# A long convolution by tables in rounded parts, its halves of the frequencies stepped one behind the other

## The chip, the cores and the metric

The kernel runs on one core of one Trainium2 chip. What counts is the device time of one execution in microseconds (us), taken as the median of several runs. Beside the runs one execution is recorded by the hardware profiler; all rows below come from it. The engines: TensorE (PE; PEld is its loading of weights), VectorE (DVE), ScalarE (ACT), GpSimd (POOL), SyncE (SP); the DMA queues that an engine feeds bear its name.

## The reference

Two layers of a backbone with a width of 1024. 512 latent tokens and 128 context tokens (640 columns in all) go through each: a gated feed-forward part, a mixer, and a second feed-forward part. The mixer splits its input between pooling, windowed attention, and an order-2 Hyena of 256 channels, whose long convolution is what the change concerns:

```python
def fft_conv(z, k):
    """z (B, L, C), k (2L, C): bidirectional convolution over the whole sequence via zero padding to 2L."""
    L = z.shape[1]
    zf = jnp.fft.rfft(z, n=2 * L, axis=1)
    kf = jnp.fft.rfft(k, n=2 * L, axis=0)
    return jnp.fft.irfft(zf * kf[None], n=2 * L, axis=1)[:, :L]

def hyena_mixer(u, sw, sb, filt, bias_d):
    uc = short_conv(u, sw, sb).astype(F32)
    v, x1, x2 = jnp.split(uc, 3, axis=-1)
    bd = bias_d.astype(F32)
    z = v
    for o, gate in enumerate((x1, x2)):
        z = gate * (fft_conv(z, filt[:, o]) + bd[o] * z)
    return z.astype(u.dtype)
```

So each layer has two long convolutions, the second on the gated result of the first.

## The kernel before

The tokens lie along the free dimension. Every large product is made in two halves of 320 columns, and as three products of rounded parts: an operand is split into a rounded `hi` (ScalarE, L294) and the rest `lo` (VectorE, L295), both of type float32r, and TensorE adds `hi*hi`, `lo*hi` and `hi*lo`. Weights come by DMA from SyncE as `raw`, are split into `whi` and `wlo`, and meet the activations `hhi`/`hlo` (or `ahi`, `phi`, ...).

In the mixer, several tasks share TensorE. Each is a generator, and a string `MIXP` (L32, walked at L1552) names the one whose next step is issued. `F` is the stream of the large products with `win` and `wout`; `A`, `X`, `Q`, `K`, `V` and `N` are attention, `P` pooling, and `C` is `hyena()`. TensorE keeps exactly the order in which its products are issued (L195 to L207); the other engines get theirs from the same program, and each engine works through its list in order. `F` asks for `C` itself once it needs its result (`phi` and `hhl`).

`C` has five steps for each of its two convolutions (`conv_step_old`, L1065), and an eleventh that splits the result into `yhi` and `ylo`:

1. The tables of the forward transform are requested (`load_full`, L256, by SyncE), the five tiles `kf` of the filter's transform are fetched, and the input is transposed on TensorE (`ztp`) and copied to `zt`.
2. The first half of the frequencies (`fi = 0`): 8 products `zf` with `zt`; ScalarE copies the odd part to `zod` (L1096), VectorE makes sum and difference `zp`, `zm`, multiplies each with the filter (`cmul`, tiles `cw` and `cy`, L966 to L971), and adds and subtracts into `pp` and `pmn` (L1104, L1105).
3. The same for `fi = 1`, then the request of the four back tables, and the context part (`zfc`, `zcs`).
4. 16 products `yt` of the back transform and the small `ytc`, scaled into `yv` by ScalarE.
5. The gate: `yu`, `yw` on VectorE.

The products of the convolution take f32 operands as they are: one instruction is one product, and the profile shows two records for it.

All these tiles, the tables among them, come from one pool of `SLOTS = 45` equal slots (`slot()`, `slot3()`), handed out in turn: whoever takes a slot waits until the last reader of its previous tile is done. The products of the convolution go to a pool of four PSUM banks (`mix`).

The program also has a second version of the step, `conv_step` (L974), which is chosen by `CONV3` (L1485) and which the kernel before does not use. It takes its tables by `load_tables` (L264); `triple` (L273) issues the three products. The program prints these functions:

Of the kernel before, what the change touches and what calls it, by code (L numbers as in the profile page):

```python
# [11 lines left out]
F32 = mybir.dt.float32  # L12
# [16 lines left out]
RCP = 300  # L29
RCP2 = 0  # L30
ORDER = "v0 v1 k q0 q1 q2 q3 xa xb v p0 p1 xc xd".split()
MIXP = "FCFFCFFFFFFCFNFCFKFFFFCQQFCQFFQFCPFFCPCFFAVAXAFAAFFCAPFXFAAPFAFFFAFFAAAFAAFFAAFAAAAXFAXFXAFFFFAFABFFBAABBFABAAFAAFFFFFFFF"  # L32
PROT = 8
AG0 = (1, 0, 2)
MIXT = 70
# [12 lines left out]
PVSKEW = 1  # L48
AHD = 2
PROP = "TGTTTTGGTGSGGGGTGTSTGTGTGSTGTGGSXTSGTSQGQDTGTQGGTTDDSTGTTQGSQGTDDTDTQQSGQQGQQDDQQDDDGTRQGSSDTSGDGGNDQNQSTTTGDGQDTSGQTDTGSGDDQGQDGTQSTQGDNGD"  # L50
CONV3 = 0
SQN = 3
TABX = 1
ADAW = (1.0, 1.25, 2.0, 0.75)
# [128 lines left out]
def hybrid_kernel(ctx: ExitStack, tc: tile.TileContext, a, depth=2, fc=22):  # L183
    nc = tc.nc
    V, S, G, DMA = nc.vector, nc.scalar, nc.gpsimd, nc.sync
# [78 lines left out]
    def load_tables(name, h, n, new=slot):  # L264

        ts = []
        for q in range(n):
            t = new(512, F32R, name="tab")
            DMA.dma_start(out=t.bitcast(F32), in_=a[name][h, q])
            ts.append(t.rearrange("p (h c f) -> p h c f", h=2, c=2))  # L270
        return ts

# [701 lines left out]
    def conv_step(l, o, z, gate, out):  # L974
        rl, rlc = filt[l]
        tf = [load_tables("fwd", 0, 4)]
        kf = filter_tiles(l, o)
        hb = PR(l, "hb")
# [15 lines left out]
        for fi in range(2):  # L994
            eo = []
            for pa in range(2):
                ps = mix(512, "zf")
                for c in range(2):
                    for i in range(2):
                        triple(ps[:, c * 256:(c + 1) * 256], [tf[fi][pa * 2 + i][:, h, c] for h in range(2)],  # L1000
                               [t[:, i, :] for t in zt[pa]], i == 0, i == 1)
                eo.append(ps)
            od = slot(512, name="zod")
            S.copy(out=od, in_=eo[1])
            zp, zm = slot(512, name="zp"), slot(512, name="zm")
            V.tensor_tensor(out=zp, in0=od, in1=eo[0], op=ALU.add)
            V.scalar_tensor_tensor(out=zm, in0=od, scalar=-1.0, in1=eo[0], op0=ALU.mult, op1=ALU.add)
            y = cmul(zp, kf[fi], o, 0)
            yp = cmul(zm, kf[2 + fi], o, 1)
            pp, pm_ = slot3(2, 256, name="pp"), slot3(2, 256, name="pmn")  # L1010
            for q in range(2):
                V.tensor_tensor(out=pp[:, q], in0=y[:, q], in1=yp[:, 1 - q], op=ALU.add)
                V.tensor_tensor(out=pm_[:, q], in0=y[:, q], in1=yp[:, 1 - q], op=ALU.subtract)
            hl = []
            for p_ in (pp, pm_):
                hl.append((slot3(2, 256, F32R, "ph"), slot3(2, 256, F32R, "pl")))
                split(p_, *hl[-1])
            pq.append(hl)
            if fi == 0:
                tf.append(load_tables("fwd", 1, 4))  # L1020
            if fi == 0:
                yield
        ti, vs = [load_tables("back", 0, 4)], []
        psc = mix(512, "zfc")
        for c in range(2):
# [119 lines left out]
    def short_conv(l, ci, u):  # L1145
        sw, sb = PR(l, "sw"), PR(l, "sb")
        t = slot(T, name="sc")
        S.activation(out=t, in_=u, func=AF.Identity, bias=sb[:, ci:ci + 1], scale=sw[:, 6 + ci:7 + ci])
        for c0, c1 in SEG:
            V.scalar_tensor_tensor(out=t[:, c0 + 1:c1], in0=u[:, c0:c1 - 1], scalar=sw[:, ci:ci + 1],  # L1150
                                   in1=t[:, c0 + 1:c1], op0=ALU.mult, op1=ALU.add)
            V.scalar_tensor_tensor(out=t[:, c0:c1 - 1], in0=u[:, c0 + 1:c1], scalar=sw[:, 12 + ci:13 + ci],
                                   in1=t[:, c0:c1 - 1], op0=ALU.mult, op1=ALU.add)
        return t
# [3 lines left out]
    def mixer(l, cur, nxt):  # L1158
# [90 lines left out]
        def need(name):  # L1249
            while name not in made:  # L1250
                next(stream)
            return made[name]
# [227 lines left out]
        def hyena():  # L1480
            zs = [short_conv(l, i, need(f"v{i}")) for i in range(2)]
            for o, (ci, ns) in enumerate(((2, ("xa", "xb")), (4, ("xc", "xd")))):
                out = []
                gate = lambda: [short_conv(l, ci + i, need(n)) for i, n in enumerate(ns)]
                yield from (conv_step if CONV3 else conv_step_old)(l, o, zs, gate, out)  # L1485
                zs = out
# [62 lines left out]
        def step(t):  # L1549
            next(tasks[t], None)  # L1550

        for t in MIXP.replace(" ", ""):  # L1552
            step(t)
# [253 lines left out]
```

## Time and profile before

| | |
|---|---|
| median of 3 runs | 2418.3 us |
| lowest and highest run | 2416.39 and 2420.72 us |
| the profiled execution, its own time | 2417.21 us |
| its span in the profile | 2415.4 us |
| TensorE busy | 2369.8 us, 98% |
| VectorE busy | 1920.3 us, 80% |
| ScalarE busy | 1094.6 us, 45% |
| GpSimd busy | 17.8 us, 1% |
| DMA, mean over the span | 112 GB/s |

The own time of the profiled execution includes what lies around its span, 1.8 us. Busy time is a sum over a stage with several limits; which engine sets the end of a stage is read from the waits and from the chain of work that ended last. Layer 0 has its mixer at about 560 to 860 us, layer 1 at about 1720 to 2020 us.

### The profile page before, as it was taken

The numbers are of one execution on the slowest core, as the hardware profiler recorded it, in microseconds if no ns is written. First come the engines' busy times: TensorE is split into PE (matmuls) and PEld (weight loads), VectorE is DVE, ScalarE is ACT, GpSimd is POOL, SyncE is SP. The second block draws the span as 40 slices with busy tenths as digits, with TensorE's granted clock in tenths as the row PEclk, the third lists the DMA queues.
The fourth block names the chain that finished last, engine by engine and source line by source line (L and its number), as shares of the span: only waits on it lengthen the run. The fifth ranks groups of instructions, "written<-read, shape, count | busy, mean of one in ns | idle before, by whom it ended". The sixth has DMA issues, their size and how long they took to land.

```text
span 2415.4 us, 41068 instructions
## 1 busy us (share of the span) xinstructions
PE 2369.8 (98%) x15576; PEld 2246.0 (93%) x15576; DVE 1920.3 (80%) x3885; ACT 1094.6 (45%) x2228; POOL 17.8 (1%) x46
## 2 busy tenths in 40 slices
PE   8999999999989999999999999999998999999999
PEld 3799999999877999999999999999987789999999
DVE  7887888986786798888889889898678678567583
ACT  4653352534345653443535435253434555335251
POOL 0000000000000000000000000000000000000000
PEclk9999999999989999999999999999998999999999
DMA  9434434353210235434343443534231022222222
GB/s 323 168 105 132 134 115 154 101 170 114 102 45 15 78 106 161 127 121 144 117 131 106 124 130 116 164 113 154 89 105 61 18 71 79 79 84 78 85 68 90
DMA packets 132646, 270.37 MB, mean 112 GB/s; under 512 B 15002, under 2 KB 24924, under 8 KB 132320
## 3 DMA queue, kind: packets, MB, share of 16 engines
q1 hardware_dynamic: 132448, 267.75, 34.5%
q8 instruction: 122, 2.00, 0.3%
q14 instruction: 76, 0.62, 0.1%
HBM read 259.56 MB, written 8.13 MB: 111 GB/s over the span
## 4 chain that ended last, share of the span: by engine, by line
PE 93%; DVE 4%; issue 1%; ACT 1%; DMA 1%; SPq 0%; POOL 0%; POOLq 0%; DVEq 0%; ACTq 0%
PE mm L204 79%; PE Z L204 5%; PE yt L204 1%; PE o L204 1%; PE pt L208 1%; PE fk L204 1%; PE mx L204 1%; PE ada L204 1%; PE zf L204 1%; PE rsb L204 0%; PE qbc L204 0%; DMA ar<-in_ada 0%; PE tot L204 0%; DMA par<-in_par 0%; PE nps L204 0%
## 5 line engine op out<-in xcount | busy, mean ns | idle before, releaser
L204 PE MATMUL mm<-hhi,whi 128*128 128x320 f32 x1440 | 448.2, 311 | 1.1 <-ACT u L1220 1.1
L204 PE MATMUL mm<-hlo,whi 128*128 128x320 f32 x1440 | 445.7, 309 | 0.0
L294 ACT CAST whi<-raw 128x512 fp32r<-128x512 f32 (+1 forms) x394 | 238.8, 607 | 456.2 <-PE mm L204 425.9
L204 PE MATMUL mm<-hhi,wlo 128*128 128x320 f32 x1440 | 445.4, 309 | 0.0
L204 PE MATMUL mm<-ahi,whi 128*128 128x320 f32 x1198 | 370.2, 309 | 0.0
L204 PE MATMUL mm<-alo,whi 128*128 128x320 f32 x1198 | 370.2, 309 | 0.0
L204 PE MATMUL mm<-ahi,wlo 128*128 128x320 f32 x1198 | 370.2, 309 | 0.0
L295 DVE TENSOR_TENSOR wlo<-raw,whi 128x512 fp32r<-128x512 f32 (+1 forms) x394 | 262.9, 670 | 77.4 <-ACT whi L294 75.2
L409 DVE CUSTOM_DVE_ANT_0 junk<-araw,condb,par 128x1024 bf16<-128x1024 f32 x240 | 307.1, 1280 | 2.2 <-DMA araw<-in_adat 0.7
L204 PEld LDWEIGHTS mm<-hhi,whi 128*128 128x128 f32 x1440 | 270.3, 188 | 6.0 <-ACT u L1220 2.8
L204 PEld LDWEIGHTS mm<-hlo,whi 128*128 128x128 f32 x1440 | 270.6, 188 | 2.0 <-issue 1.8
L204 PEld LDWEIGHTS mm<-hhi,wlo 128*128 128x128 f32 x1440 | 270.3, 188 | 1.4 <-issue 1.4
L204 PE MATMUL mm<-thi,whi 128*128 128x320 f32 x864 | 267.0, 309 | 0.0
L204 PE MATMUL mm<-tlo,whi 128*128 128x320 f32 x864 | 267.0, 309 | 0.0
L204 PE MATMUL mm<-thi,wlo 128*128 128x320 f32 x864 | 267.0, 309 | 0.0
L204 PEld LDWEIGHTS mm<-ahi,whi 128*128 128x128 f32 x1198 | 224.9, 188 | 0.0
L204 PEld LDWEIGHTS mm<-ahi,wlo 128*128 128x128 f32 x1198 | 224.9, 188 | 0.0
L204 PEld LDWEIGHTS mm<-alo,whi 128*128 128x128 f32 x1198 | 224.9, 188 | 0.0
L294 ACT CAST whi<-ex 128x512 fp32r<-128x512 f32 x216 | 134.2, 621 | 186.9 <-PE mm L204 173.3
L295 DVE TENSOR_TENSOR wlo<-ex,whi 128x512 fp32r<-128x512 f32 x216 | 148.9, 689 | 31.7 <-ACT whi L294 27.2
L294 ACT CAST whi<-ws 128x512 fp32r<-128x512 f32 x144 | 89.4, 621 | 162.2 <-PE mm L204 123.1
L204 PEld LDWEIGHTS mm<-tlo,whi 128*128 128x128 f32 x864 | 162.2, 188 | 0.0
(263 smaller groups left out, 4713.6 us busy)
## 6 DMA issues: line engine op xcount, KB each, us to landing
araw<-in_adat SPq DMA_DIRECT2D x120, 512.0 KB, 3.6
raw<-in_wgu SPq DMA_DIRECT2D x208, 256.0 KB, 3.0
ex<-in_wgu SPq DMA_DIRECT2D x144, 256.0 KB, 2.7
raw<-in_wd SPq DMA_DIRECT2D x128, 256.0 KB, 2.7
raw<-in_win SPq DMA_DIRECT2D x56, 256.0 KB, 2.8
ar<-in_ada SPq DMA_DIRECT2D x48, 256.0 KB, 5.4
raw<-in_wd SPq DMA_DIRECT2D x64, 192.0 KB, 2.6
tab<-in_tfi SPq DMA_DIRECT2D x32, 256.0 KB, 4.1
```

The lines of the kernel that those rows point to most:

```text
L204: cls.order(nc.tensor.matmul(**k))
L208: cls.order(nc.tensor.transpose(**k))
L294: S.copy(out=hi, in_=src)
L295: V.tensor_tensor(out=lo, in0=src, in1=hi.bitcast(F32), op=ALU.subtract)
L409: V.tensor_tensor_reduce(out=junk, in0=raw, in1=condb[:, r], scale=1.0, scalar=bias(l, g)[:, s, c, r:r + 1], op0=ALU.mult, op1=ALU.add, ac ...
```

## The change

Three lines change:

```diff
-MIXP = "FCFFCFFFFFFCFNFCFKFFFFCQQFCQFFQFCPFFCPCFFAVAXAFAAFFCAPFXFAAPFA...
+MIXP = "FCFFCFFFFFFCFNFCFKFFFFCQQFCQFFQFCCPFAFAPAFCAVFAXFFCFAPFXFAAPFA...
...
-CONV3 = 0
+CONV3 = 1
...
             t = new(512, F32R, name="tab")
-            DMA.dma_start(out=t.bitcast(F32), in_=a[name][h, q])
+            G.dma_start(out=t, in_=a[name][h, q])
             ts.append(t.rearrange("p (h c f) -> p h c f", h=2, c=2))
```

`G` is GpSimd. With `CONV3 = 1` the steps of `C` run as `conv_step`, cut here to what differs:

```python
    def conv_step(l, o, z, gate, out):
        tf = [load_tables("fwd", 0, 4)]
...
        zt = [(slot3(2, 256, F32R, name="zt"), slot3(2, 256, F32R, name="ztl")) for _ in range(2)]
...
            split(ps, *(t.rearrange("p a b -> p (a b)") for t in zt[pa]))
...
        yield
        for fi in range(2):
...
                        triple(ps[:, c * 256:(c + 1) * 256], [tf[fi][pa * 2 + i][:, h, c] for h in range(2)],
                               [t[:, i, :] for t in zt[pa]], i == 0, i == 1)
...
            for p_ in (pp, pm_):
                hl.append((slot3(2, 256, F32R, "ph"), slot3(2, 256, F32R, "pl")))
                split(p_, *hl[-1])
            pq.append(hl)
            if fi == 0:
                tf.append(load_tables("fwd", 1, 4))
            if fi == 0:
                yield
        ti, vs = [load_tables("back", 0, 4)], []
...
        yield
        yt = [mix(512, "yt") for _ in range(2)]
        for pa in range(2):
            if pa == 1:
                ti.append(load_tables("back", 1, 4))
            for c in range(2):
...
                        triple(yt[c][:, pa * 256:(pa + 1) * 256], [t[:, q, cs] for t in pq[fi][pa]],
                               [tab[:, h] for h in range(2)], n == 0, n == 3)
```

Each of a step's 8 table tiles of 256 KB becomes two, 16 in all (a tile now holds `hi` and `lo` of half of what it held): four forward ones per half of the frequencies, four back ones per half of the output. They are requested in four lots, by GpSimd. The transposed input is split (`zt`, `ztl`), and so are `pp` and `pmn` (`ph`, `pl`): two and four splits a step. Each product becomes three. Over the kernel these are 128 products that become 384, 24 more subtractions on VectorE, 16 more operations on ScalarE, and 64 table requests where there were 32. In `MIXP` the eighth `C` (the second convolution's second half of the frequencies) now stands directly behind the seventh, and the `C` behind it comes after a few steps of `A`, `F` and `P`.

The order on TensorE in the second convolution of layer 0, before. `zf_7273` is the end of `fi = 0`, `zf_7493` and `zf_7498` are `fi = 1`, `tab_7148` to `tab_7154` the forward tables, `mm` a product of `F`:

```order
L204 MATMUL zf_7273<-zt_7167,tab_7152 128x256
L204 MATMUL zf_7273<-zt_7167,tab_7154 128x256
L204 MATMUL zf_7493<-zt_7166,tab_7148 128x256
L204 MATMUL zf_7493<-zt_7166,tab_7150 128x256
L204 MATMUL zf_7498<-zt_7167,tab_7152 128x256
L204 MATMUL zf_7498<-zt_7167,tab_7154 128x256
L204 MATMUL mm_7371<-hhi_6075,whi_7375 128x320
```

Both halves stand together and use the same four tables (16 products in all); behind them come 48 products of `F`, `zfc`, and 54 more products before the first `yt`.

The same place in the change: the end of `fi = 0` (`zf_7385`), the products of `F` behind it, and the begin of `fi = 1` (`zf_7442`), which takes a new table, `tab_7434`:

```order
L204 MATMUL zf_7385<-zt_7268,tab_7254 128x256
L204 MATMUL mm_7590<-hhi_6075,whi_7594 128x320
...
L204 MATMUL mm_7591<-hhi_6113,wlo_7625 128x320
L204 MATMUL zf_7442<-zt_7266,tab_7434 128x256
L204 MATMUL zf_7442<-ztl_7267,tab_7434 128x256
L204 MATMUL zf_7442<-zt_7266,tab_7436 128x256
```

Now 48 products of `F` lie between the halves. Further on, the end of `fi = 1` (`zf_7455`) and the begin of the back products (`yt_7801`, with `tab_7504`, `ph` and `pl`):

```order
L204 MATMUL zf_7455<-zt_7268,tab_7440 128x256
L204 MATMUL yt_7801<-tab_7504,ph_7426 128x256 x2
L204 MATMUL yt_7801<-tab_7504,pl_7427 128x256
L204 MATMUL yt_7801<-tab_7506,ph_7426 128x256 x2
L204 MATMUL yt_7801<-tab_7506,pl_7427 128x256
```

Between the last `zf` and the first `yt` nothing is left; the second half of the output follows 72 products later. On GpSimd, which had no DMA before, the requests of the second and third lot follow each other, then the memsets of the pool mixer (`pl`), with the engines and DMA queues whose semaphores each waits on:

```order
L269 DMA tab_7434<-in_fwd 128x512 [waits DMASW4_49,DMAHW3_49,DVE_49,Activation_49]
L269 DMA tab_7436<-in_fwd 128x512 [waits DMASW5_49,DVE_49,PE_49]
L269 DMA tab_7438<-in_fwd 128x512 [waits DMAHW6_49,DMASW6_49,DVE_49]
L269 DMA tab_7440<-in_fwd 128x512 [waits DMASW7_49,DMASW4_49,PE_49]
L269 DMA tab_7504<-in_back 128x512 [waits DMASW0_49,DMASW7_49,DVE_49,PE_49]
L269 DMA tab_7506<-in_back 128x512 [waits DMASW1_49,DVE_49]
L269 DMA tab_7508<-in_back 128x512 [waits DMASW2_49,DVE_49,Activation_49]
L269 DMA tab_7510<-in_back 128x512 [waits DMASW3_49]
L1166 MEMSET pl_7655 128x8 [waits DMASW2_49,PE_49]
```

Each request waits for the last user of its slot, and, since GpSimd takes them in turn, for the one ahead of it. The previous users are tiles of the convolution itself: for `tab_7434` VectorE's `pmn` of `fi = 0`, for `tab_7440` TensorE's last product with `tab_7434`, for `tab_7504` VectorE's `cy` of `fi = 1`.

## Rows read from the trace of the kernel before

**Rows 1.** The page: the span, section 1 (busy time, share, instructions), section 4 (last chain).

```profile
span 2415.4 us, 41068 instructions
...
PE 2369.8 (98%) x15576; PEld 2246.0 (93%) x15576; DVE 1920.3 (80%) x3885; ACT 1094.6 (45%) x2228; POOL 17.8 (1%) x46
...
PE 93%; DVE 4%; issue 1%; ACT 1%; DMA 1%; SPq 0%; POOL 0%; POOLq 0%; DVEq 0%; ACTq 0%
```

**Rows 2.** Busy us of each engine by stretch, then mean granted clock, DMA share, GB/s.

```profile
core 0: us, PE busy (x) PEld busy (x) DVE busy (x) ACT busy (x) POOL busy (x), PEclk, DMA share, GB/s
637.00:720.00 83.00, 74.21 (x399) 61.44 (x399) 71.81 (x173) 35.04 (x84) 0.56 (x8) 0.92 0.25 84
...
860.00:1720.00 860.00, 854.88 (x5808) 852.62 (x5807) 751.83 (x1400) 379.84 (x729) 5.25 (x7) 1.00 0.40 127
```

**Rows 3.** Waits of TensorE in 560 to 760: us in total, times, longest.

```profile
PE pt L208 <- DVE sc L1353: 3.6, 1, 3.6
...
PE yt L204 <- DMA tab<-in_tfi: 3.5, 2, 3.1
```

**Rows 4.** Timeline of TensorE: start, us, operation; then a group (busy, mean ns).

```profile
575.49 0.31 PE L204 MATMUL mm<-hhi,kwh 128*128 128x320 f32 x1
...
577.54 0.31 PE L204 MATMUL mm<-hhi,wlo 128*128 128x320 f32 x1
...
654.49 7.17 PE L204 MATMUL zf<-zt,tab 128*128 128x256 f32 x32 [1.05 <-ACT zt L1077]
...
L204 PE MATMUL zf<-zt,tab 128*128 128x256 f32 x128 | 28.8, 380 | 2.1 <-ACT zt L1077 2.1
```

**Rows 5.** Timeline of ScalarE and VectorE behind the first step's first half.

```profile
586.03 0.59 ACT L1096 COPY zod<-zf 128x512 f32<-128x512 f32 x1 [4.74 <-PE zf L204]
...
591.06 0.42 DVE L970 TENSOR_TENSOR cy<-cw 128x256 f32<-128x256 f32 x1
...
592.41 0.76 DVE L1105 TENSOR_TENSOR pmn<-cy,cy 128x256 f32<-128x256 f32 x2
```

**Rows 6.** Timeline in the second step, then the DMA view and line 260's landings.

```profile
677.98 0.42 DVE L970 TENSOR_TENSOR cy<-cw 128x256 f32<-128x256 f32 x1
...
678.48 2.37 SPq L260 DMA_DIRECT2D tab<-in_tfi  x4
...
681.21 2.04 PE L204 MATMUL yt<-tab,pp 128*128 128x256 f32 x4 [3.05 <-DMA tab<-in_tfi]
...
683.72 2.04 PE L204 MATMUL yt<-tab,pp 128*128 128x256 f32 x4 [0.46 <-DMA tab<-in_tfi]
...
tab<-in_tfi SPq DMA_DIRECT2D x32, 256.0 KB, 4.1
...
DMA to landing us min/median/max: 2.8/4.6/6.3
```

**Rows 7.** Timeline of the second step's tail.

```profile
691.96 0.61 PE L204 MATMUL ytc<-cst,cy 128*128 128x128 f32 x4
...
709.86 0.78 PE L208 MATMUL pt<-ident,sc 128*128 128x128 f32 x2 [3.58 <-DVE sc L1353]
...
710.43 1.27 PE L204 MATMUL pm<-pd,par 128*128 128x320 f32 x2
...
711.92 3.02 PE L204 MATMUL pm<-pd,par 128*128 128x320 f32 x6
...
713.66 1.34 ACT L294 CAST yhi<-yw 128x640 fp32r<-128x640 f32 x2
...
714.54 0.70 PE L204 MATMUL mm<-phi,whi 128*128 128x320 f32 x2
```

**Rows 8.** Timeline of VectorE, two splits of a weight tile.

```profile
593.08 1.29 DVE L295 TENSOR_TENSOR wlo<-raw,whi 128x512 fp32r<-128x512 f32 x2
```

**Rows 9.** Stretches at half clock (columns as in rows 2).

```profile
680.29:687.11 6.82, 5.44 (x12) 3.96 (x13) 6.63 (x16) 1.37 (x3) 0.28 (x4) 0.50 0.57 166
...
707.60:714.42 6.82, 4.57 (x11) 3.13 (x12) 6.67 (x15) 4.64 (x11) 0.00 (x0) 0.50 0.00 1
```

More of the change, by code (lines that the diff above doesn't have):

```diff
@@ L31 @@
 ORDER = "v0 v1 k q0 q1 q2 q3 xa xb v p0 p1 xc xd".split()
-MIXP = "FCFFCFFFFFFCFNFCFKFFFFCQQFCQFFQFCPFFCPCFFAVAXAFAAFFCAPFXFAAPFAFFFAFFAAAFAAFFAAFAAAAXFAXFXAFFFFAFABFFBAABBFABAAFAAFFFFFFFF"
+MIXP = "FCFFCFFFFFFCFNFCFKFFFFCQQFCQFFQFCCPFAFAPAFCAVFAXFFCFAPFXFAAPFAFFFAFFAAAFAAFFAAFAAAAXFAXFXAFFFFAFABFFBAABBFABAAFAAFFFFFFFF"
 PROT = 8
```

## The prediction

> **What bounds the kernel now.** I read the page first: TensorE is busy 98% of the span, and the chain that ended last runs through it for 93% [rows 1]. So a change counts by what it does to TensorE's time: shorter products, or new waits in front of them. Then the busy time by stretch [rows 2]. In the feed-forward stretches (860 to 1720) nothing of the change stands and TensorE is busy 854.88 of 860 us. The long convolution lies in the mixer, 577 to 860 in layer 0. In 637 to 720, where its second step runs, TensorE is busy only 74.21 of 83 us, VectorE 71.81 (87%), and the granted clock falls to a mean of 0.92. That is the one stretch with slack on TensorE and none on VectorE, and the change puts its work there. The waits view [rows 3] says who is waited for: the rescaled attention scores `sc` on VectorE, and the back tables `tab` that a DMA brings, 3.5 us in two waits. Thus the tables are late already, at one place, by one request.
>
> **The change part by part** (per layer; both layers hold the same two steps).
>
> *Three products for one.* In the profile an old f32 product is two records: 32 records take 7.17 us, of which one's tail is 0.38, so (7.17 - 0.38) / 31 = 0.219 each and 0.438 a product [rows 4]. Of the rounded products of 320 columns 15 follow each other from 575.49 to 577.54, 2.05 / 14 = 0.146 us apart [rows 4]; one of 256 columns costs between 256/320 of that, 0.117, and all of it, 0.146. I take 0.12, since these rows stream at a steady pitch: 3 x 0.12 = 0.36, saved 0.078. A layer has 64 old products (32 `zf`, 32 `yt`): **-5.0 us**, bounds -5.6 and nothing.
>
> *Second step, tables of the second half of the frequencies.* Before, four forward tables serve both halves and the 16 `zf` products run in one go. Now four new ones are fetched at the end of the first half, into slots of a pool of 45 that is full: the first takes the slot whose last reader is VectorE's `pmn` of the first half. That chain, from `zod` to the end of `pmn`, took 593.17 - 586.03 = 7.14 us where nothing held it up [rows 5]. A table landed 2.8 to 6.3 us after its issue, median 4.6 [rows 6]; I take the median. TensorE has 48 products between the halves, 48 x 0.146 = 7.0 us. So the first `zf` of the second half waits 7.14 + 4.6 - 7.0 = 4.7 (2.9 to 6.4). The fourth table's slot is freed only by TensorE's last use of the first one; six products and `zfc`, about 1 us, lie between: 3.6 (1.8 to 5.3). Directly behind the second half now come the back products `yt`, whose first table takes a slot freed by VectorE's `cy`, 591.48 - 586.03 = 5.45 us after `zod` [rows 5], with nothing between on TensorE: 5.45 + 4.6 = 10.05 (8.25 to 11.75). Before, 20 us of other products lay there (from the end of `zf`, 661.66 [rows 4], to 681.21), and still the tables cost 3.05 + 0.46 = 3.5 us, because their request at 678.48 followed `cy` by half a microsecond [rows 6]. Sum 18.35 - 3.5 = **+15** (9 to 20).
>
> *The tail of the step.* Before, 22.6 us pass from `ytc` (691.96) to the first product of `phi` (714.54), with 3.58 us of waiting for `sc` among them [rows 7]. Since `yhi` (713.66) stands among the `phi` casts on ScalarE, these are bound to the gate behind `yt`, a list of VectorE work that the change leaves as it was. TensorE now has less to do there: 48 products (7.0), four `pm` (1.27 + 3.02 = 4.3 at half clock, 2.1 at full), and 5 `vt` with the small `sc` products (about 2): some 12 to 13 us. The rest, 22.6 - 13 = 9.6, is waiting, 3.6 of it old: **+6** (0, if VectorE's list there is shortened by as much, to 9.6).
>
> *Splits.* Six more subtractions on VectorE per step, 12 per layer; two took 1.29 us [rows 8], so 7.7 us on an engine 87% busy. The casts beside them go to ScalarE, 35.04 of 83 us busy [rows 2], at nothing; if that cover is gone they cost as much as the subtractions. Of the 7.7 I count **+5** (0 to 7.7): most of it falls into the chains above, just before a product needs its low part.
>
> *Other tables.* In the first step 60 products (8.8 us) cover the second half's tables, against 7.14 + 4.6, or + 6.3 at most, and some slots come free earlier, with `zm`. The back tables of the second output half stand on GpSimd behind the pool mixer's memsets, which wait for slots too; 72 products (10.5 us) cover them. Between nothing and 4.6 (chain and slowest landing over cover) plus one landing of 4.1: **+4.5** (0 to 8.7). The 32 requests that leave SyncE [rows 6] free its queue, but the weights behind it are early already: nothing.
>
> *The clock.* After the waits of 3.05 and 3.58 us TensorE's granted clock was 0.50 (1.2 instead of 2.4 GHz) for 6.82 us each [rows 9]; TensorE was busy 5.44 and 4.57 us in these, so each lost about half of that, 2.3 to 2.7. Two more waits of this length, at 2 us each: **+4** (0 to 6.8, were TensorE busy throughout).
>
> *Sum*: -5 + 15 + 6 + 5 + 4.5 + 4 = +29.5 a layer, +59. The profiled execution took 2417.2, so 2476.2; the median of the three runs lies 1.1 above it: **2477 us**. All terms at their low ends give -5.6 + 9 = +3.4 a layer (2425), all at the high ones 20 + 9.6 + 7.7 + 8.7 + 6.8 = +53 (2524); they don't fall to one end together.
>
> **The rivals.**
>
> *A. Loads that GpSimd issues land later.* Before, no DMA came from GpSimd (its 46 instructions are memsets and small arithmetic [rows 1]), so no row here prices one. If a table lands at the slowest 6.3 in place of 4.6, four waits a layer grow by 1.7, 6.8 us, and each longer gap takes its half-clock stretch along (some 3 us more in two of them): +14 a layer, **2505 us**. For it: GpSimd gets one request done after the other, each behind its own slot. Against: the transfers are of the same 256 KB.
> The Trainium skill (DMA: Bandwidth & Descriptors, section SWDGE vs HWDGE vs iDMA) says that for loads from GpSimd a core there computes the descriptors in software, and that a load into float32r always casts and can come from nowhere else. Its section Specifications puts the first byte at about 1 us, against 0.6 for SyncE's: an estimate from it is 0.4 x 4 x 2 = 3 us on the sum. No run shown yet has such a load. A second rule speaks against the change: the Trainium skill (SBUF - State Buffer, section SBUF: two separate sides) warns that some of VectorE's faster copies lock GpSimd out of writing descriptors, so that the load seems blocked. VectorE is busy at the moment of the requests here, but with two-input subtractions and additions; by that rule rival A would be the result.
>
> *B. The tables are in time: faster.* If slots come free at least 4.6 us before a product needs its table, no new wait arises, the splits run beside TensorE, and only the -5 stays: 2 x -5 = -10, **2408 us**. It decides at the cover: 7.14 + 4.6 us is 80 products, where 48 stand; for `yt` it would take 10.05 us of other work, where none stands. For it speaks that VectorE has 11 us free in the stretch, against it both orders.
>
> *C. Tables in time, splits not hidden*: the -5 is eaten by 7.7 of subtraction: +2.7 a layer, **2424 us**, slower by a little.
>
> *D. No difference*: the order's move does nothing and the terms cancel, within 4.8 us. Three products for one are plain in the new order of TensorE, so that the change does not do what it says is nearly excluded; the move of the eighth `C` behind the seventh is plain too.
>
> **How the numbers follow.** The forecast has 0.62, A 0.23, C 0.06, B 0.06, D 0.03. A measurement of this kernel tells some 0.2% (4.8 us) from no change; its three runs spread over 4.3. Faster by more than that is B, 0.06; within it D, 0.03; slower A, C and the forecast, 0.91. The range: from the forecast downwards the uncertain terms (tail, splits, other tables, clock: 19.5 a layer) at barely half, 2477 - 37 = 2440; upwards through A with a little of the tail's high end, 2515. Left out are B, C and D (0.15) and the outer ends.
>
> **What would show it.** In the changed profile: `zf` and `yt` products as three records of 0.12 us pitch; waits of `zf` and of `yt` on the DMA of `tab`, 4 to 10 us each, four or five a layer, where [rows 3] has 3.5 in all; the stretch of the second step longer by 20 us or more, with new half-clock stretches behind the gaps; a first product of `phi` late behind `yhi`; and feed-forward stretches unchanged. A median landing near 6 us for the new loads is A. If TensorE's waits for `tab` sum to under 5 us a layer, the prediction is wrong and it is B or C: C if TensorE then waits for `ztl`, `pl` or `phi` instead.

## The result, and the profile after

| | before | changed |
|---|---|---|
| median | 2419.51 us (4 runs) | 2486.15 us (4 runs) |
| lowest and highest | 2416.39, 2421.19 | 2483.3, 2491.8 |
| ratio, 95% interval | | 1.028 [1.0258, 1.0302] |
| the profiled execution, span | 2415.4 | 2485.9 |

The change costs 66.6 us. The forecast was 2477 us, 59 more, in a range of 2440 to 2515. The page of the changed kernel (span, busy time, two of its DMA queues, and the new loads), to be held against [rows 1] and the line of the DMA view in [rows 6]:

```profile
span 2485.9 us, 41511 instructions
PE 2379.6 (96%) x15704; PEld 2260.8 (91%) x15704; DVE 1937.6 (78%) x3909; ACT 1104.0 (44%) x2244; POOL 53.4 (2%) x110
...
q1 hardware_dynamic: 127840, 259.36, 32.5%
q0 software_dynamic: 9216, 16.78, 2.5%
...
tab<-in_fwd POOLq DMA_DIRECT2D x32, 256.0 KB, 3.2
```

TensorE is idle 2485.9 - 2379.6 = 106.3 us, where it was idle 45.6: 60.7 of the 70.5 us by which the span grew are waiting, 9.8 are busy time, though each product of the convolution got shorter: part of that work runs at half the clock, as the rows on the clock below show. Next, the busy time by stretch of the changed kernel: the second step's stretch, and one of feed-forward work, moved by the 35.2 us that a layer now takes longer:

```profile
637.00:720.00 83.00, 57.09 (x308) 49.26 (x306) 59.23 (x130) 20.78 (x44) 8.90 (x24) 0.84 0.31 94
```

```profile
895.20:1755.20 860.00, 853.47 (x5797) 851.33 (x5797) 750.43 (x1393) 377.82 (x724) 6.75 (x10) 1.00 0.40 128
```

The feed-forward part is what it was [rows 2]. In 637 to 720 TensorE does 57.09 us where it did 74.21, and VectorE 59.23 where it did 71.81: the engine that I took for the full one is less busy than before. Both wait for something. TensorE's timeline of layer 0 says for what (in brackets how long it stood idle, and what it waited for):

```profile
665.59 0.64 PE L204 MATMUL mm<-hhi,whi 128*128 128x320 f32 x1 [5.13 <-ACT u L1220]
...
677.30 0.36 PE L204 MATMUL zf<-zt,tab 128*128 128x256 f32 x1 [2.70 <-DMA tab<-in_fwd]
...
679.83 0.58 PE L204 MATMUL zf<-zt,tab 128*128 128x256 f32 x1 [1.93 <-DMA tab<-in_fwd]
...
684.61 0.39 PE L204 MATMUL zf<-zt,tab 128*128 128x256 f32 x1 [0.79 <-DMA tab<-in_fwd]
...
694.95 0.77 PE L204 MATMUL yt<-tab,ph 128*128 128x256 f32 x2 [9.00 <-DMA tab<-in_back]
...
697.54 0.77 PE L204 MATMUL yt<-tab,ph 128*128 128x256 f32 x2 [0.76 <-DMA tab<-in_back]
...
717.22 0.69 PE L204 MATMUL mm<-khi,qhi 64*128 64x384 f32 x1 [2.62 <-DVE m L1398]
...
720.24 0.80 PE L204 MATMUL yt<-tab,ph 128*128 128x256 f32 x2 [0.87 <-DMA tab<-in_back]
...
746.60 0.63 PE L204 MATMUL mm<-phi,whi 128*128 128x320 f32 x1 [8.97 <-ACT phi L1195]
```

These nine waits are 32.8 us of the layer. Before, the same stretch held 3.05 and 0.46 at `yt`, 3.58 at `pt` [rows 6, 7] and 0.57 at the first `mm` behind `zf`, 7.7 in all; the last of them, from the trace of the kernel before:

```profile
662.23 0.42 PE L204 MATMUL mm<-hhi,whi 128*128 128x320 f32 x1 [0.57 <-ACT u L1220]
```

Why the tables come late is seen on ScalarE, VectorE and GpSimd, each from its own timeline:

```profile
664.59 0.62 ACT L294 CAST qhi<-rp 128x512 fp32r<-128x512 f32 x1 [3.35 <-DVE rp L1307]
665.12 0.74 ACT L1220 COPY u<-mm 128x320 f32<-128x320 f32 x2
665.75 0.60 ACT L1004 COPY zod<-zf 128x512 f32<-128x512 f32 x1
...
685.99 0.58 ACT L1004 COPY zod<-zf 128x512 f32<-128x512 f32 x1 [10.88 <-PE zf L204]
```

```profile
672.14 0.76 DVE L1013 TENSOR_TENSOR pmn<-cy,cy 128x256 f32<-128x256 f32 x2
...
686.61 0.69 DVE L1006 TENSOR_TENSOR zp<-zod,zf 128x512 f32<-128x512 f32 x1 [10.78 <-ACT zod L1004]
...
691.36 0.42 DVE L971 TENSOR_TENSOR cy<-cw 128x256 f32<-128x256 f32 x1
```

```profile
673.42 0.53 POOL L269 DMA_DIRECT2D tab<-in_fwd  x1 [28.12 <-ACT ph L294]
674.63 1.06 POOL L269 DMA_DIRECT2D tab<-in_fwd  x2 [0.67 <-PE mm L204]
681.77 0.53 POOL L269 DMA_DIRECT2D tab<-in_fwd  x1 [6.08 <-PE zf L204]
691.97 1.06 POOL L269 DMA_DIRECT2D tab<-in_back  x2 [9.67 <-DVE cy L971]
693.65 1.05 POOL L269 DMA_DIRECT2D tab<-in_back  x2 [0.62 <-ACT ph L294]
```

The first table of the second half is requested at 673.42, half a microsecond after `pmn` ended (672.90); the row names ScalarE's `ph`, the cast of `pp`, which ended at 672.88, and in layer 1 the same wait is put down to `pmn`. The fourth waits for TensorE's own `zf`, the back tables for `cy`: 691.97, 0.2 us after its end (691.78). GpSimd had been ready for 28 and 10 us. What is late is the slot, not the load.

One sentence of the part on the kernel before is wrong: TensorE does not keep the order of issue there, since the switch for it (`fixed`, L189) is never set; the scheduler that builds the program orders it. All orders shown are the built ones, so the terms of the prediction stand.

### The profile page after: what moved, and what is told of

Read it like the earlier page. It is cut to its first block, busy times and chain, and to the rows that moved or that the text cites. A ratio compares the mean times of both kernels' runs of the same rounds, so it can differ in the third digit from the quotient of the medians.

```text
span 2485.9 us, 41511 instructions
## 1 busy us (share of the span) xinstructions
PE 2379.6 (96%) x15704; PEld 2260.8 (91%) x15704; DVE 1937.6 (78%) x3909; ACT 1104.0 (44%) x2244; POOL 53.4 (2%) x110
## 5 line engine op out<-in xcount | busy, mean ns | idle before, releaser
L204 PEld LDWEIGHTS mm<-thi,wlo 128*128 128x128 f32 x864 | 162.2, 188 | 0.0
```

What stands on the lines that cost most here:

```text
L204: cls.order(nc.tensor.matmul(**k))
```

## The experiments

Each ratio is to runs of the kernel before, taken beside those of the run. "Order" is the `MIXP` of the change or the old one, "tables" how many tiles a step loads.

| run | order | tables | median us | ratio to before, 95% |
|---|---|---|---|---|
| the change | new | 16 | 2486.15 | 1.0280 [1.0258, 1.0302] |
| m1_order_only | new | 8, f32 | 2446.81 | 1.0119 [1.0100, 1.0137] |
| c1_parts_only | old | 16 | 2474.86 | 1.0224 [1.0204, 1.0244] |
| e1_fwd_early | new | 16 | 2468.17 | 1.0202 [1.0187, 1.0217] |
| e2_all_early | new | 16 | 2457.10 | 1.0154 [1.0137, 1.0171] |
| e3_old_fwd_early | old | 16 | 2455.77 | 1.0143 [1.0119, 1.0168] |
| s2_lo_on_act | new | 16 | 2482.06 | 1.0247 [1.0222, 1.0272] |
| s1_no_sub | new | 16 | 2471.00 | 1.0206 [1.0183, 1.0229] |
| t1_phi_first | new | 16 | 2485.05 | 1.0264 [1.0243, 1.0285] |
| k1_fill | new | 16 | 2488.09 | 1.0280 [1.0258, 1.0302] |
| h1_new_reuse | new | 8 | 2461.91 | 1.0172 [1.0155, 1.0188] |
| h2_old_reuse | old | 8 | 2448.68 | 1.0114 [1.0091, 1.0137] |
| h4_old_leanest | old | 8, fewest tiles | 2415.01 | 0.9977 [0.9964, 0.9990] |

### The two halves of the change apart

```diff
 # m1_order_only: the change with
-CONV3 = 1
+CONV3 = 0
 # c1_parts_only: the change with the old order
-MIXP = "...FFQFCCPFAFAPAFCAVFAXFFCFAPF..."
+MIXP = "...FFQFCPFFCPCFFAVAXAFAAFFCAPF..."
```

> New order of the steps, old f32 convolution (one product, four tables for both halves, requests by SyncE). Theory (late tables and the shortened tail): no waits of zf for tables are left, since all four come at the start of the step; yt directly behind the second half still waits for its first back table, some 5 to 9 us, and phi some 9 us where pt waited 3.6; so 9 to 14 us a layer, 2438 to 2447 us. Rival (the three products with their splits and new tables are the whole cost, the order is free): 2414 to 2424 us.

> Old order of the steps, convolution in three products with its 16 tables from GpSimd. Theory: the eighth C stands farther behind the seventh, but the tables are still requested only when VectorE frees their slots, so zf waits 5 to 8 us a layer, and yt 5 to 10 us; phi's wait of 9 us goes back to pt's 3.6; 17 to 28 us a layer, 2452 to 2475 us, below the change. Rival (order is what costs): 2405 to 2425 us. If order and parts add up plainly, this run's excess and that of the order alone sum to the change's 67 us.

Measured: the order alone costs 27.1 us (2446.81 against 2419.7), the parts alone 55.2; both at the upper ends of the theory. Their sum, 82.3, is 16 more than the change costs, so the two share waits. TensorE's timeline of m1_order_only:

```profile
660.73 0.42 PE L204 MATMUL mm<-hhi,whi 128*128 128x320 f32 x1 [0.58 <-ACT u L1220]
...
673.48 3.20 PE L204 MATMUL yt<-tab,pp 128*128 128x256 f32 x6 [4.60 <-DVE pp L1104]
...
699.09 0.69 PE L204 MATMUL mm<-khi,qhi 64*128 64x384 f32 x1 [3.46 <-DVE m L1398]
...
725.33 0.64 PE L204 MATMUL mm<-phi,whi 128*128 128x320 f32 x1 [8.97 <-ACT phi L1195]
```

and of c1_parts_only:

```profile
664.53 0.64 PE L204 MATMUL mm<-hhi,whi 128*128 128x320 f32 x1 [5.14 <-ACT u L1220]
...
676.17 0.55 PE L204 MATMUL zf<-zt,tab 128*128 128x256 f32 x1 [2.40 <-DMA tab<-in_fwd]
...
702.43 0.77 PE L204 MATMUL yt<-tab,ph 128*128 128x256 f32 x2 [10.93 <-DMA tab<-in_back]
...
714.82 0.80 PE L204 MATMUL yt<-tab,ph 128*128 128x256 f32 x2 [4.88 <-DMA tab<-in_back]
...
738.06 0.78 PE L208 MATMUL pt<-ident,sc 128*128 128x128 f32 x2 [3.43 <-DVE sc L1353]
```

The waits for `phi` and `m` belong to the order: the f32 convolution has them too. The waits for `tab` belong to the parts, in either order. `yt`'s wait is in both, and is most of what they share: over the two layers TensorE waits at `yt` for 7.9 us before, 9.2 with the order alone, 31.9 with the parts alone and 20.9 in the change, 12.3 less than the two excesses would add up to. The theory holds; the rivals (one half is free) both fall.

### Tables requested earlier

```diff
 # e1_fwd_early (on the change) and e3_old_fwd_early (on c1_parts_only)
-        tf = [load_tables("fwd", 0, 4)]
+        tf = [load_tables("fwd", i, 4) for i in range(2)]
...
-            if fi == 0:
-                tf.append(load_tables("fwd", 1, 4))
 # e2_all_early: e1_fwd_early, and
             pq.append(hl)
+            if fi == 0:
+                ti = [load_tables("back", 0, 4)]
...
-        ti, vs = [load_tables("back", 0, 4)], []
+        vs = []
...
+        ti.append(load_tables("back", 1, 4))
         yt = [mix(512, "yt") for _ in range(2)]
         for pa in range(2):
-            if pa == 1:
-                ti.append(load_tables("back", 1, 4))
```

> The change, with the forward tables of both halves requested together at the start of the step. Theory: the 10.5 us in which zf waited for tab in the two layers go, and the half-clock stretches behind them; 12 to 27 us less than the change, 2459 to 2474 us; yt's wait of 9 us a layer and phi's of 9 us stay. Rival (the wait only moves on to yt or phi, which VectorE's chain sets): within 6 us of the change.

> Old order of the steps, three products, forward tables of both halves requested together at the start. Theory (order and parts cost by different waits, so that they can be undone one by one): the zf waits of the run with the old order (3.4 us a layer, and the half-clock stretches behind them) go, 8 to 20 us less than its 2474.9, so 2455 to 2467 us. Rival (yt's wait grows by what zf's shrinks): 2470 us or more.

> As the run before, and the first back tables requested at the end of the first half of the frequencies, the others at the start of the back products. If the tables alone hold yt up, its 9 us a layer go too: 18 us and half-clock time less than the run before, 2435 to 2450 us. Rival: the fifth product of yt needs ph of the second half, which in the change is written 692.5 to 693.8, 1.2 to 2.5 us before the table lands at 694.95, so VectorE's chain takes the wait over: only 2 to 5 us a layer are gained, 4 to 10 us less than the run before.

Measured: e1_fwd_early 18 us less than the change, e3_old_fwd_early 19 less than c1_parts_only. As the theory had it, no `zf` waits for a table any more, in either order. More than I had foreseen hangs on it: in the built order of both, the 48 `zf` products of the two halves stand together again, and 48 others (102 in the old order) lie between them and `yt`. So the late tables had also taken the cover from `yt`; yet its wait stayed, 10.29 us in e1_fwd_early, because its own table follows VectorE's chain wherever it stands: it is requested at 683.56, when `cy` is done. Its timeline on TensorE and on GpSimd:

```profile
686.65 0.77 PE L204 MATMUL yt<-tab,ph 128*128 128x256 f32 x2 [10.29 <-DMA tab<-in_back]
```

```profile
683.56 1.10 POOL L269 DMA_DIRECT2D tab<-in_back  x2 [36.78 <-DVE cy L971]
```

e2_all_early gains 11.1 more, between the theory's 18 and the rival's 4 to 10. Its timeline on TensorE shows the rival's mechanism plainly:

```profile
674.10 0.48 PE L204 MATMUL yt<-tab,ph 128*128 128x256 f32 x2 [0.95 <-DMA tab<-in_back]
...
681.50 1.01 PE L204 MATMUL yt<-tab,ph 128*128 128x256 f32 x3 [5.52 <-ACT ph L294]
```

The tables are there, `yt` begins, and at the fifth product it waits 5.52 us for the data itself, `ph` of the second half. Set against the 9.76 us in the change, these 6.47 leave 3.3 a layer to the table alone; the rest is VectorE's chain, which nothing here shortens.

### The splits: work or slots

```diff
 # s2_lo_on_act
-            split(ps, *(t.rearrange("p a b -> p (a b)") for t in zt[pa]))
+            for t in zt[pa]:
+                S.copy(out=t.rearrange("p a b -> p (a b)"), in_=ps)
...
-                split(p_, *hl[-1])
+                for t in hl[-1]:
+                    S.copy(out=t, in_=p_)
 # s1_no_sub
-        zt = [(slot3(2, 256, F32R, name="zt"), slot3(2, 256, F32R, name="ztl")) for _ in range(2)]
+        zt = [(slot3(2, 256, F32R, name="zt"),) * 2 for _ in range(2)]
...
-            split(ps, *(t.rearrange("p a b -> p (a b)") for t in zt[pa]))
+            S.copy(out=zt[pa][0].rearrange("p a b -> p (a b)"), in_=ps)
...
-                hl.append((slot3(2, 256, F32R, "ph"), slot3(2, 256, F32R, "pl")))
-                split(p_, *hl[-1])
+                hl.append((slot3(2, 256, F32R, "ph"),) * 2)
+                S.copy(out=hl[-1][0], in_=p_)
```

> The change with the low parts of the convolution's activations written by ScalarE as second copies instead of VectorE's subtractions (so the rounding corrections are left out of the output); all tiles, slots and products stay. Theory (my term, VectorE's 12 subtractions a layer cost 5 us): 2474 to 2478 us. Rival (VectorE idles 10.8 us before zp in this stretch, the subtractions are hidden): 2482 to 2488 us, no different from the change.

> The change without its 24 subtractions and without the 24 tiles that hold them: every product that would take the low part of an activation takes the high part again, so the output leaves the rounding corrections of the convolution's activations out. Theory (my term: splits cost 5 us a layer as work on VectorE): 2474 to 2478 us, and as low as the run in which ScalarE makes the low parts. Rival (it is the slots that count: six tiles fewer a step in a pool of 45, so tables get their slots earlier): 10 to 25 us below that other run, with waits for tab shrinking.

In both runs, and in h4_old_leanest below, the high part stands where the low one would, so the output is not that of the convolution; only the time is read.

Measured: with all 24 subtractions taken from VectorE and every tile kept, 2482.06. That is 4.1 us less than the change by the medians and 8 by the ratios, whose intervals overlap. So 2 to 4 us a layer where my term had 5, not clear of noise, and with 24 copies more on ScalarE in it: the expected 2474 to 2478 is missed, but the price of the subtractions as work is not pinned down. With the tiles gone as well, 2471.0, another 11.1 less. From the second step of layer 0, the second half's `zod` on ScalarE, the request of the back tables on GpSimd and the first `yt` on TensorE, each from its engine's own timeline, in s2_lo_on_act and then in s1_no_sub:

```profile
686.62 0.59 ACT L1005 COPY zod<-zf 128x512 f32<-128x512 f32 x1 [8.54 <-PE zf L204]
...
692.60 1.05 POOL L269 DMA_DIRECT2D tab<-in_back  x2 [9.69 <-DVE cy L971]
...
696.03 0.77 PE L204 MATMUL yt<-tab,ph 128*128 128x256 f32 x2 [9.44 <-DMA tab<-in_back]
```

```profile
674.72 0.59 ACT L1004 COPY zod<-zf 128x512 f32<-128x512 f32 x1 [3.59 <-PE zf L204]
...
678.76 1.05 POOL L269 DMA_DIRECT2D tab<-in_back  x2 [10.21 <-DVE cy L971]
...
682.11 1.83 PE L204 MATMUL yt<-tab,ph 128*128 128x256 f32 x7 [6.99 <-DMA tab<-in_back]
```

From `zod` to the request it is 5.98 us with the tiles, as in the change (691.97 - 685.99), and 4.04 without them: the slots that come next are then freed by an earlier `cy` of the chain. So a split is dear for the slot that its result holds. s1_no_sub also makes 24 copies fewer on ScalarE than s2_lo_on_act, so not all of the 11.1 us need be the slots'.

### The tail

```diff
 # t1_phi_first
-            while len(hhl) < 2:
-                step("C")
             for _ in pools:
                 pass
+            while len(hhl) < 2:
+                step("C")
```

> The change with the pool mixer's last steps ahead of the eleventh C, so that the phi casts stand ahead of yhi on ScalarE. Theory (the tail is VectorE's list up to the gate, yw): the first product of phi no longer waits, but the products of hhi behind it wait for ylo instead; 0 to 5 us less than the change, 2481 to 2487 us. Rival (the place of phi in ScalarE's queue is the cause): both waits of 9 us go, 18 us and some half-clock time, 2460 to 2468 us.

Measured: 2485.05, within the spread of the change. The wait only changes its name (TensorE's timeline):

```profile
738.65 0.41 PE L204 MATMUL mm<-phi,whi 128*128 128x320 f32 x1 [2.01 <-ACT phi L1195]
...
744.89 0.63 PE L204 MATMUL mm<-plo,whi 128*128 128x320 f32 x1 [5.46 <-DVE plo L1196]
```

`phi` is early, but `plo` is VectorE's, behind the same gate. What sets the tail is VectorE's list, as the prediction had it, not a place in ScalarE's queue.

### The clock

```diff
 # k1_fill
         yt = [mix(512, "yt") for _ in range(2)]
+        for n in range(28 if o else 0):
+            PE.matmul(out=yt[0][:, 0:128], lhsT=ones, rhs=tcx[:, 0, :], start=True, stop=True)
```

> The change with 28 idle products (f32, 128 columns, of two constant tiles, into the bank of yt, overwritten by its first real product) in each layer's second step ahead of yt; 22 of them stand in the place where TensorE waits 9 us, 6 ahead of it. They need no new data and end, at some 0.24 us each, before the table lands. Theory (the gap brings the half-clock stretch behind it, 13.66 us with 7.83 us of work): up to 3.9 us a layer are gained, 2477 to 2484 us, and that stretch shrinks. Rival (clock is not what the gap costs, or the 3 to 4 us of waiting that are left bring the stretch as well): within 3 us of the change, or slower.

Measured: 2488.09, no gain, so the rival's result. From the first `yt` to the first product of `phi`, in the change and then with the filling:

```profile
694.95:746.60 51.65, 37.42 (x198) 32.27 (x198) 33.15 (x90) 22.49 (x58) 2.67 (x12) 0.80 0.18 52
```

```profile
693.23:745.08 51.85, 37.42 (x197) 31.65 (x197) 32.93 (x90) 22.40 (x58) 2.68 (x12) 0.83 0.18 52
```

The wait at `yt` was cut to 4.14 us. The half-clock stretch there shrank from 13.66 us (689.88 to 703.54) to this:

```profile
692.64:699.46 6.82, 5.51 (x24) 5.28 (x25) 2.25 (x6) 0.98 (x5) 0.43 (x3) 0.50 0.41 114
```

Most of what went lay in the gap itself: behind the first `yt` the half clock lasted 6.2 us instead of 8.6. That little brought nothing: the stretch from `yt` to `phi` takes the same 52 us, with the same 37.42 us of TensorE work. Its end is set elsewhere, as t1_phi_first says too.

### What a table more costs

```diff
 # h1_new_reuse (on the change) and h2_old_reuse (on c1_parts_only)
-                tf.append(load_tables("fwd", 1, 4))
+                tf.append(tf[0])
...
-                ti.append(load_tables("back", 1, 4))
+                ti.append(ti[0])
 # h4_old_leanest: h2_old_reuse without low parts (as s1_no_sub), and
-            pp, pm_ = slot3(2, 256, name="pp"), slot3(2, 256, name="pmn")
+            pp, pm_ = slot3(2, 256, F32R, name="pp"), slot3(2, 256, F32R, name="pmn")
...
-                hl.append((slot3(2, 256, F32R, "ph"),) * 2)
-                S.copy(out=hl[-1][0], in_=p_)
+                hl.append((p_, p_))
```

> The change with the first lot of forward tables used for both halves of the frequencies and the first lot of back tables for both halves of the output: 8 tables a step as before instead of 16; products and splits stay, and the output is that of wrong tables. Theory (the doubled tables are the cost of the parts): next to the run of the new order with the f32 convolution (2446.8), less 10 us of products, plus what splits cost, 2436 to 2450 us; no zf waits for tab, phi's 9 us stay. Rival (splits and the loads from GpSimd cost by themselves): 2460 us or more.

> The same eight tables a step in the old order of the steps. Theory: next to the kernel before, less 10 us of products, plus a later first yt (its tables wait for VectorE as before) and plus splits: 2412 to 2432 us, against 2474.9 with sixteen tables. Rival: 2445 us or more.

> Old order; eight tables a step (the first lots used twice, as in the runs before); no low parts and no copies of pp and pmn: the products take the rounded tile three times, so a step holds as many tiles of the pool as in the kernel before, and what is left of the change is three float32r products for one and loads from GpSimd. The output is that of wrong tables and leaves the corrections out. Theory (what the parts cost is the slots that their tables and low parts take): the kernel before less 10 us of products, plus the 3 to 5 us that an earlier first yt waits more a layer, 2408 to 2426 us. Rival (loads from GpSimd or the float32r products cost by themselves): 2435 us or more, near the 2448.7 with low parts.

Measured: eight tables fewer a step gain 24.2 us in the new order and 26.2 in the old one. Both stay above my theory, 2461.91 and 2448.68, on the rivals' side: 15 us above m1_order_only and 28 above the kernel before. That left two candidates, the low parts' tiles and the new kind of load and product. h4_old_leanest decides: with no more tiles a step than before, three products and loads from GpSimd give 2415.01 us, 0.9977 [0.9964, 0.9990] of the kernel before. Its TensorE and GpSimd:

```profile
685.83 1.83 PE L204 MATMUL yt<-tab,pp 128*128 128x256 f32 x7 [3.84 <-DMA tab<-in_back]
```

```profile
682.86 1.07 POOL L269 DMA_DIRECT2D tab<-in_back  x2 [10.64 <-DVE cy L971]
```

The loads and the products cost nothing; they give 5 of the 10 us that were reckoned, with 1.9 us a layer more of waiting in it (11.1 us for 9.2 in 560 to 760). What remains of h2_old_reuse, 33.7 us, is the low parts, the copies and their tiles; this run does not part the tiles from the work of filling them. The theory had this right in kind and too small: I had counted only the tables' slots there.

One more comparison bears on this. e1_fwd_early and e3_old_fwd_early hold all sixteen tables, but request the forward ones at the start of the step, and they lie only 6.3 and 7.1 us above h1_new_reuse and h2_old_reuse, which hold eight. So most of the 24 to 26 us is the price of the place of the request, and little of it that of the slots as such.

## Why the prediction was right, and where not

**The mechanism was right.** Tables requested behind VectorE's chain, for want of a slot at the place where they are asked for: each link is in the trace, and the runs that requested the forward ones earlier took `zf`'s waits away. The forecast fell 9 us short, and that it came so near is in part luck: it put the second step, the other tables and the splits too high and left out two waits, as follows.

- *Products, -5 a layer*: right in the pitch, 24 `zf` start 0.12 us apart. h4_old_leanest, which keeps little but the products, is the one run that is faster than before, by 5 us of the 10.
- *Second step, +15*: the chain from `zod` to the end of `pmn` took 672.90 - 665.75 = 7.15 us (forecast 7.14), that to the end of `cy` 691.78 - 685.99 = 5.8; the forecast's 5.45 ended with the first half of the last `cy`, one instruction early. Two sizes were wrong. The first back table took 3.0 us (691.97 to 694.95) and the fourth forward one 2.8 (681.77 to 684.61), not 4.6, which is the median of all loads of line 260, five others among them; the DMA view had 4.1 for the tables alone [rows 6]. And the 48 products between the halves took 9.0 us (665.59 to 674.60), not 7.0, since the first of them ran at half clock behind the wait for `u`. So `zf` waited 5.4 instead of 8.3, and `yt` 9.8 instead of 10.05; the term measured 5.4 + 9.8 - 3.5 = 11.7.
- *A wait that I left out*: 5.13 us for `u`, the copies that free PSUM for the 48 products between the halves. Before, both halves' `zf` (7.17 us) stood ahead of these products [rows 4] and covered the copies; now one half of 24 products does. The prediction had the halves apart and did not ask what the second had hidden: +4.6 in layer 0 and 3.2 in layer 1. It is the late tables that part them, not the order: c1_parts_only, in the old order, waits 5.14, and m1_order_only, in the new one with its halves together, 0.58. The cover is not all of it. TensorE could go on 10.6 us after the last product ahead of `zf` instead of 8.8, because on ScalarE the copies stand behind a `qhi` that waits for VectorE, which now makes `ztl` ahead of that; e1_fwd_early, whose halves stand together too, still waits 2.91.
- *The tail, +6*: right, 8.97 (and 0.52 for `p`) for 3.58, also in m1_order_only; t1_phi_first confirms that it is VectorE's list. The 2.62 us for `m`, which the order brings as well, stood in no term.
- *Splits, +5*: as work not borne out, 2 to 4 and not clear of noise (s2_lo_on_act). VectorE was not the full engine that I took it for: it stood idle 10.8 us ahead of `zp`. The tiles have a price of their own (s1_no_sub, whose back tables are requested 1.9 us sooner behind `zod`); h2_old_reuse against h4_old_leanest gives 16.8 us a layer for both together.
- *Other tables, +4.5*: 0.87 in this order; nothing of note in the first step.
- *The clock, +4*: the half-clock stretches grew as said, and more, but k1_fill took 2.4 us of half clock from behind the first `yt` and got no time for it. The rows of layer 0 in the change:

```profile
662.58:669.40 6.82, 3.81 (x14) 3.82 (x15) 5.61 (x12) 1.76 (x4) 0.00 (x0) 0.50 0.41 143
679.64:683.06 3.42, 3.23 (x14) 3.15 (x15) 0.00 (x0) 0.00 (x0) 0.53 (x1) 0.50 0.05 8
689.88:703.54 13.66, 7.83 (x33) 7.59 (x34) 7.60 (x18) 3.90 (x9) 2.39 (x8) 0.50 0.30 77
717.19:724.02 6.83, 5.93 (x23) 5.42 (x24) 1.66 (x8) 0.37 (x1) 1.84 (x4) 0.50 0.61 183
741.09:751.32 10.23, 4.72 (x16) 4.03 (x17) 7.63 (x13) 3.13 (x6) 0.00 (x0) 0.50 0.00 0
```

41 us at half clock with 25.5 us of work, against 13.64 us with 10.0 of work before [rows 9]. Half of the difference in work, 7.8 us, is the most that this can cost a layer; how much of it is paid stays open, since the filling reached only one of the five stretches and only part of that.

Added up for layer 0, the terms that were measured give -5 + 11.7 + 4.6 + 5.9 + 2.6 + 0.9 = 20.7 us (the -5 as forecast), where the kernel got 33.3 a layer slower. Smaller waits of TensorE in 560 to 760 add some 3 and the clock at most 7.8; the rest is not assigned.

Two sums of the prediction do not come out. The 37 us below the forecast are nearly all of the uncertain terms (19.5 a layer, 39 in both), not barely half of them; and A's terms, 6.8 and twice 3, give 12.8 a layer and not 14.

**The rivals.** A, loads from GpSimd that land later, falls: they landed 2.7 to 5.7 us after issue, median 3.2, where SyncE's tables had 4.1, and all loads of line 260 2.8 to 6.3 [rows 6]. The Trainium skill (DMA: Bandwidth & Descriptors, section SWDGE vs HWDGE vs iDMA) says that loads from GpSimd take longer to set up; no such cost shows here from issue to landing, only the issue itself is longer, 0.54 us against a median of 0.42. The Trainium skill's warning that VectorE may block such loads (SBUF - State Buffer, section SBUF: two separate sides) is about some of VectorE's faster copies, and was not put to the test: at 673 and 692 us VectorE was running two-input operations, of which the same section says that they did not stall such loads; so A does not follow from that rule, as the prediction had it. No landing here shows a block. B and C asked for tables in time, which they were not; e2_all_early came nearest, and there the data took the tables' place. D falls with the measured 1.028.

## What to carry to other kernels

Where a pool is full, count a new operand by the slot that it takes and by who frees that slot, before its bytes or its arithmetic: here 8 tables more cost 24 to 26 us, of which all but 6 or 7 went when half of them were requested earlier, and 24 subtractions, moved to ScalarE, some 4 to 8 and not clear of noise, while the same products without more tiles gained 5. A request that waits for a slot follows the chain that it should run ahead of; ask for it a step earlier if the pool allows, and then look whether the data itself is ready any sooner. When a group of products is moved, look at what it had covered, not only at what it waits for.

## What the runs showed that I had not expected

A load issued by GpSimd into float32r landed in 3.2 us (median of 64), sooner than the 4.1 of SyncE's loads of the same 256 KB into the same pool. That is no lead of GpSimd's in general: SyncE's weights of 256 KB landed in 2.7 to 3.0 in the kernel before. And order and parts were not additive, 82.3 us apart against 66.6 together, because both lay bare the same wait at `yt`, which VectorE's chain sets.
